# Delta rule: turning values and outputs, and spreading samples' keys, on VectorE, ScalarE and GpSimd instead of TensorE

## The chip, the core and the metric

The program runs on one core of one Trainium2 chip. A core has five engines with a queue each: PE (TensorE, matrix products), DVE (VectorE, elementwise work and 32x32 transposes), ACT (ScalarE, elementwise functions and copies), POOL (GpSimd, elementwise work and some of the DMAs) and SP (SyncE, which here only issues DMAs). Each engine works through its own instructions in the order in which the program issues them and waits, where it has to, for results of the others. The metric is the device time of one execution in microseconds (us); less is better.

## The reference

The program computes one layer of a decoder for one new sequence of 256 tokens (the prompt) and 8 samples of 4 tokens each, 288 tokens together, in float32. What this change touches is the gated delta rule of 8 heads with 128 channels each. For a chunk of tokens with state S, it computes

```
u = T @ (vc * bc)                    # T: inverse of a unit triangular matrix made from keys and decays
w = T @ (kb * jnp.exp(gcum)[..., None])
v_new = u_c - w_c @ S
o = qd @ S + a_c @ v_new
S = S * jnp.exp(gl)[..., None] + jnp.einsum('bhcd,bhce->bhde', kd, v_new)
```

The prompt's 256 tokens are 4 chunks of 64, one after the other. Each of the 8 samples has its own state per head, which its 4 tokens update once. Before and after it stand large matrix products: an input projection (2048 to 11,280 columns), output projections and a feed-forward block with 8192 hidden columns.

## The kernel before

**The stream of blocks.** All large products are cut into 496 blocks of 512 KB of weights (4 groups of 128 rows by 256 columns). Weights in float32 are not multiplied as they are: ACT rounds a block to a shorter format (`split_hi`, L185, tile `hi`), DVE computes what is left over (`split_lo`, L141 by the helper `tt`, tile `lo`), and PE makes three products for each piece (`matmuls`, L211, L212, L214): high by high, high by low, low by high. A block is 24 such products. The main loop goes over blocks i. In iteration i it issues, in this order: `split_hi(i+3)`; one step of the side work, `next(sgen)`; one step of the sample work, `next(aux[0])`; `split_lo(i+3)`; what is due after earlier blocks (`due`: results taken out of PSUM); and then block i's products. `hi` and `lo` have 4 buffers each, so `split_hi(i+3)` can start when PE is done with block i-1.

**Side work.** The delta rule has little arithmetic but a long chain of dependent steps. It is a Python generator, `gdn(G)`, for two groups of 4 heads, G=0 and then G=1. Every `yield` in it ends a step, and one step is issued per block. So the PE instructions of a step stand in PE's queue between block i-1 and block i, and the number of `yield`s between a result and the PE instruction that uses it is written out by hand: it decides how many blocks of PE time the other engines have for it. The samples' part is a second generator inside it, `sample()`, put into `aux` and stepped beside it. When G=0 is through and `aux` is empty, G=1 begins (`side`, L1431 to L1436).

**What gdn does, by lines.** The keys are transposed by PE (L1035), their norms taken, decays made (L1079 to L1102), key-by-key products made (L1111). DVE scales these (`nM`, `aT`). From L1137 to L1144 DVE prepares small 8x8 systems; ACT and POOL split them (`mx`, L1174, L1175); PE sums them (L1181, tile n88); DVE solves them in a chain of about 16 small instructions (L1183 to L1188) and transposes the result (L1189, `Tf`). Three `yield`s later PE begins to merge the blocks into the inverse (`pairs`, L1170, twice for each of two sizes, with ACT's copy L1195 between; then L1208 and L1223), which ends in `U128`. Then comes the loop over the 4 chunks (L1331 to L1372): PE multiplies keys by the state (L1336, p1), DVE subtracts (L144 by the helper `stt`), PE multiplies by `U128` (L1348, p2), DVE scales, PE makes the state's update and the output (L1356 and L1359, p3 and p4), DVE or ACT adds.

**What the change touches in it.** Values lie in `vf` with channels on the partitions and are turned by 8 PE transposes (L1324), with DVE scaling them on the way out of PSUM. The outputs are turned back by 8 PE transposes (L1396), with ACT copies (L1399) into `ao`, which the z blocks read. The sample part needs keys and new values spread to 4 row groups, one for each head: ACT writes the keys 4 times (L1053, `wide`), PE transposes them (L1058) into `kr`; later ACT writes the matrix `Us` 4 times (L1274) and PE makes 4 products from it (L1281). `lows` (L1234 to L1239) rounds such a tile and leaves high or low parts in their row groups. POOL multiplies the samples' states by their decays (L1231, `decay`) and spreads new values with a mask (L1297, `vm`); PE makes the states' updates (L1308).

**Beside it.** While G=0 runs, blocks 24 to 47 produce the keys, queries and values of G=1. After every fourth block a result is due: in the first step after it, and in the next, POOL clears and fills a border (L271, L272), ACT copies out of PSUM (L273, L274) and makes the first product of a convolution of 4 taps (L276, which waits for L272), DVE makes the other three (L144, 128x312), POOL saves a tail (L279). In the third, ACT applies SiLU (L286 to L293). These steps are 28, 29, 30; 32, 33, 34; up to 48, 49, 50. While G=1 runs, the blocks are those of the gated short convolution, with DVE work due in 3 of 12 steps (L141, L144, L344).

```
                act.mul(c, pad[:, 0:312], hw[:, ti, 24:25])
                for j in range(1, 4):
                    stt(c, pad[:, j:j + 312], hw[:, ti, 24 + j:25 + j], c, MUL, ADD)
```

## Time and profile before

| what | value |
|---|---|
| time, median of 3 runs | 1677.83 us (1677.59 to 1677.97) |
| time of the profiled execution | 1677.98 us |
| its span, first to last instruction | 1676.1 us |
| PE busy | 1666.5 us |
| DVE, ACT, POOL busy | 971.6, 733.9, 126.9 us |
| granted TensorE clock | 0.998 |
| G=0, from the first key transposes (L1035) to the output transposes (L1396) on the chain | 80.67 to 251.50 us |
| G=1, the same | 258.87 to 407.37 us |

Times inside the profile count from the first instruction. The chain of waits follows back from the last instruction what each one waited for; a line of it gives start, duration, engine, tile, line and count. The timeline of an engine gives start, duration, line, operation, what is written from what, its shape, and in brackets how long the engine had been idle and who ended that. Groups of instructions give busy time, the mean of one in ns, and idle time before them.

### The profile page before, as it was taken

What the parts mean: (1) busy time and instruction counts of PE and PEld (TensorE: products, weight loads), DVE (VectorE), ACT (ScalarE), POOL (GpSimd) and SP (SyncE); (2) the same over time, 40 slices, a digit from 0 to 9 for tenths busy, and PEclk for the clock granted to TensorE, in tenths of its full rate; (3) what the DMA queues carried; (4) which work ended last, traced back from release to release, by engine and by line L of the source; (5) the groups of instructions that cost most, each with busy time, mean ns of one, the idle gap of its engine ahead of it and who ended that gap; (6) DMA issues with size and microseconds to landing.
All of it is one profiled execution on the core that took longest, in us unless ns stands there. A gap on an engine that the chain in (4) does not pass through costs nothing.

```text
span 1676.1 us, 31314 instructions
## 1 busy us (share of the span) xinstructions
PE 1666.5 (99%) x13245; PEld 1653.1 (99%) x13245; DVE 971.6 (58%) x1244; ACT 733.9 (44%) x1029; POOL 126.9 (8%) x210
## 2 busy tenths in 40 slices
PE   9999999999999999999999999999999999999998
PEld 8999999999999999999999999999999999999997
DVE  5687967676444445457776666544444444444465
ACT  6775545335443333334444445443334433344343
POOL 1223311232200000000000000000000000000000
PEclk9999999999999999999999999999999999999999
DMA  8554466436555555555565555555555555555552
GB/s 274 160 176 152 137 197 189 153 114 201 172 168 167 165 164 163 165 167 162 161 204 165 167 167 163 167 163 164 165 166 167 168 166 164 163 164 166 165 162 83
DMA packets 276035, 279.36 MB, mean 167 GB/s; under 512 B 13779, under 2 KB 270996, under 8 KB 275888
## 3 DMA queue, kind: packets, MB, share of 16 engines
q1 hardware_dynamic: 271782, 265.87, 51.0%
q0 software_dynamic: 3824, 11.16, 2.4%
q8 instruction: 104, 1.70, 0.4%
q10 hardware_dynamic: 288, 0.33, 0.1%
q14 instruction: 37, 0.30, 0.1%
HBM read 269.83 MB, written 7.48 MB: 165 GB/s over the span
## 4 chain that ended last, share of the span: by engine, by line
PE 99%; DMA 1%; DVE 0%; issue 0%; SPq 0%; ACT 0%; POOL 0%
PE acc L211 31%; PE acc L214 31%; PE acc L212 31%; PE g L1170 0%; PE g L1336 0%; DMA xs<-in_x_sample_dram 0%; PE g L1356 0%; PE g L1359 0%; PE g L909 0%; DMA xr<-in_x_prompt_dram 0%; PE g L1161 0%; PE g L1111 0%; PE g L1308 0%; PE g L1348 0%; PE g L1035 0%; PE g L628 0%
## 5 line engine op out<-in xcount | busy, mean ns | idle before, releaser
L141 DVE TENSOR_TENSOR lo<-raw,hi 128x1024 fp32r<-128x1024 f32 (+1 forms) x503 | 614.1, 1224 | 593.4 <-ACT hi L185 592.5
L185 ACT CAST hi<-raw 128x1024 fp32r<-128x1024 f32 (+1 forms) x499 | 519.0, 1042 | 805.4 <-PE acc L212 705.6
L211 PE MATMUL acc<-xh,hi 128*128 128x288 f32 x1408 | 399.4, 299 | 0.3 <-ACT hi L1449 0.3
L212 PE MATMUL acc<-xl,hi 128*128 128x288 f32 x1408 | 394.4, 295 | 0.0
L214 PE MATMUL acc<-xh,lo 128*128 128x288 f32 x1408 | 302.1, 295 | 0.0
L212 PE MATMUL acc<-dl,hi 128*128 128x288 f32 (+1 forms) x1024 | 287.7, 295 | 0.0
L211 PE MATMUL acc<-dh,hi 128*128 128x288 f32 (+1 forms) x1024 | 287.6, 295 | 0.0
L211 PE MATMUL acc<-hh,hi 128*128 128x288 f32 x1024 | 287.4, 295 | 0.0
L212 PE MATMUL acc<-hl,hi 128*128 128x288 f32 x1024 | 287.2, 295 | 0.0
L211 PEld LDWEIGHTS acc<-xh,hi 128*128 128x128 f32 x1408 | 264.6, 188 | 2.5 <-issue 1.0
L212 PEld LDWEIGHTS acc<-xl,hi 128*128 128x128 f32 x1408 | 264.6, 188 | 0.9
L214 PEld LDWEIGHTS acc<-xh,lo 128*128 128x128 f32 x1408 | 226.0, 188 | 0.0
L214 PE MATMUL acc<-hh,lo 128*128 128x288 f32 x1024 | 222.6, 296 | 0.0
L214 PE MATMUL acc<-dh,lo 128*128 128x288 f32 (+1 forms) x1024 | 219.8, 296 | 0.0
L211 PEld LDWEIGHTS acc<-dh,hi 128*128 128x128 f32 x1024 | 193.3, 189 | 0.1
L212 PEld LDWEIGHTS acc<-dl,hi 128*128 128x128 f32 x1024 | 192.8, 188 | 0.1
L211 PEld LDWEIGHTS acc<-hh,hi 128*128 128x128 f32 x1024 | 192.4, 188 | 0.0
L212 PEld LDWEIGHTS acc<-hl,hi 128*128 128x128 f32 x1024 | 192.2, 188 | 0.0
L214 PEld LDWEIGHTS acc<-hh,lo 128*128 128x128 f32 x1024 | 165.1, 188 | 0.0
L214 PEld LDWEIGHTS acc<-dh,lo 128*128 128x128 f32 x1024 | 164.6, 188 | 0.0
L211 PE MATMUL acc<-mh,hi 128*128 128x288 f32 x256 | 72.1, 298 | 0.0
L212 PE MATMUL acc<-ml,hi 128*128 128x288 f32 x256 | 71.7, 295 | 0.0
(414 smaller groups left out, 1479.8 us busy)
## 6 DMA issues: line engine op xcount, KB each, us to landing
raw<-in_w_in_dram SPq DMA_DIRECT2D x175, 512.0 KB, 3.5
raw<-in_w_up_dram SPq DMA_DIRECT2D x128, 512.0 KB, 3.7
raw<-in_w_down_dram SPq DMA_DIRECT2D x128, 512.0 KB, 3.5
raw<-in_w_o_dram SPq DMA_DIRECT2D x32, 512.0 KB, 3.6
raw<-in_w_a_out_dram SPq DMA_DIRECT2D x16, 512.0 KB, 3.6
raw<-in_w_b_out_dram SPq DMA_DIRECT2D x16, 512.0 KB, 3.6
S<-in_state_gdn_dram POOLq DMA_DIRECT2D x8, 512.0 KB, 6.4
out_dram<-S POOLq DMA_DIRECT2D x8, 512.0 KB, 4.7
```

Source lines behind the costliest of these rows:

```text
L141: dve.tensor_tensor(out=out, in0=a, in1=b, op=op)
L185: act.copy(his[i][:, k:k + step], raw[i][:, k:k + step])
L211: pe.matmul(ps[:, t, 0:n], wh, xh_, start=st, stop=False)
L212: pe.matmul(ps[:, t, 0:n], wh, xl_, start=False, stop=False)
L214: pe.matmul(ps[:, t, 0:n], l[:, k, t * P:(t + 1) * P], xh_, start=False, stop=en)
```

## The change

1. **Values.** The 8 PE transposes and 2 DVE products after the sample part's start are gone. Right after L1111, DVE turns `vf` in 32x32 blocks in one instruction (128x1024) into the room of `U128`; ACT moves the blocks to their places in 16 copies (32x256), four in each of four steps (`move_v`); DVE scales all in one 128x1024 product, just ahead of n88. The clearing of `U128` by POOL moves behind that.
2. **Outputs.** DVE turns `o` in one 128x1024 instruction, ACT moves it in 16 copies (32x256), eight in each of two steps.
3. **Keys of the samples.** `wide`, its 4 PE transposes, the norms of the fourfold tile and its factors (`srep`, `rsc`) are gone; `kr` is one 128x128 tile copied from a transpose that was there already.
4. **Spreading.** `lows`, the second `wide` and the 4 PE products are gone. `quarters` rounds the tile (ACT), takes the rest (DVE), and copies 16 pieces (32x128) to their row groups: all 16 by POOL for the keys; for the new values 8 by POOL and 8 by ACT.
5. **Steps.** The `sample` generator gets longer by two steps up to its `po` and its pieces move among them; one step between the merge matrix `Us` and its use is gone. The chunk loop starts one step earlier in both groups and, for G=0, loses the extra `yield` after each chunk. So G=0 ends, and G=1 starts, five steps earlier.

```diff
+        v = T([P, 4, 2, P], "v")
+        vt = U128.rearrange("p q x -> p (q x)")
+        dve.transpose(out=vt, in_=vf.rearrange("p r c a x -> p (r c a x)"))
+        vtv = vt.rearrange("p (r c a e) -> p c r a e", r=2, c=4, a=4)
+        def move_v(j):
+            for w in range(4):
+                act.copy(v[32 * w:32 * w + 32, :, :, 32 * j:32 * j + 32], vtv[32 * j:32 * j + 32, :, :, w])
...
-        yield
+        move_v(0)
+        yield
+        move_v(1)
...
         gps.tensor_tensor(out=mx[:, 1], in0=Xf, in1=mx[:, 0], op=SUB)
+        move_v(2)
         yield
         spread_kq(1)
-        yield
+        move_v(3)
+        yield
+        vq = v.rearrange("p c r x -> p (c r) x")
+        tt(vq, vq, bc(nr[:, 0:8], P), MUL)
+        gps.memset(U128, 0.0)
         n88 = gtile()
...
+        def quarters(out, src, side_):
+            act.copy(hl[:, 0], src)
+            tt(hl[:, 1], src, hl[:, 0], SUB)
+            for hh in range(4):
+                for w in range(4):
+                    low = w // 2 if side_ == 0 else w % 2
+                    d, r = out[32 * w:32 * w + 32, hh], hl[32 * hh:32 * hh + 32, low]
+                    if side_ and w % 2:
+                        act.copy(d, r)
+                    else:
+                        gps.tensor_copy(d, r)
+                if hh % 2:
+                    yield
...
             dve.transpose(out=Ts, in_=Us)
             yield
-            yield
+            yield from quarters(kr3, kr, 0)
...
             dve.copy_predicated(Us, msk("s"), pqs[:, 0:P])
-            lows(kr3, kr, 0)
-            yield
-            act.copy(wide, four(Us))
             yield
             pv_ = gtile()
             pe.matmul(pv_[:, 0:P], Us, vs, start=True, stop=True)
             act.mul(vns, pv_[:, 0:P], sc[:, 1:2])
-            vtr = gtile()
-            for hh in range(4):
-                pe.matmul(vtr[:, hh * P:hh * P + P], rep4[:, hh * P:hh * P + P], vs, start=True, stop=True)
-            vr = sqr[:, 0:512].rearrange("p (h d) -> p h d", h=4)
-            tt(vr, vtr.rearrange("p (h d) -> p h d", h=4), bc(rsc[:, 1], P), MUL)
             v3 = pl.tile([P, 4, P], F32R, tag="U", name=nm("v3"))
-            lows(v3, vr, 1)
+            yield from quarters(v3, vns, 1)
...
-        for u in range(2):
-            vt = gtile()
-            for w in range(4):
-                pe.transpose(vt[:, w * P:(w + 1) * P], vf[:, w % 2, 2 * u + w // 2].rearrange("p a x -> p (a x)"), ident)
...
             yield
-            if G == 0:
-                yield
         gps.dma_start(A["new_gdn_prompt"][0, 0, hs].rearrange("h d e -> d h e"), S)
...
+        ot = v.rearrange("p c r x -> p (c r x)")
+        dve.transpose(out=ot, in_=o.rearrange("p c r x -> p (c r x)"))
+        otv = ot.rearrange("p (c r j x) -> p j r c x", c=4, r=2, j=4)
         yield
+        for w in range(4):
+            for j in range(4):
+                h = 4 * G + 1 - w // 2
+                ao = gd["ao"][32 * j:32 * j + 32, 1, h:4 * G + 4:2, 0:NP_].rearrange("p r (c t x) -> p t r c x", c=4, t=2)
+                act.copy(ao[:, w % 2], otv[32 * w:32 * w + 32, j])
+            if w == 1:
+                yield
```

More of the change, by code (lines that the diff above doesn't have):

```diff
@@ L972, in gates @@
                 gps.tensor_copy(gw[64 - 64 * par:128 - 64 * par, half], qv[src, par, 0])
-        srep = cp.tile([P, 2, 8], F32, name="srep")
-        act.activation(srep[:, 0], q[:, 136:144], AF.Exp)
-        act.copy(srep[:, 1], q[:, 144:152])
         s4 = cp.tile([P, 4, 8], F32, name="s4")
@@ L984, in gates @@
         dve.tensor_scalar(out=sx[:, 3, :], in0=s1[:, 0, :], scalar1=-1.0, scalar2=None, op0=MUL)
-        G_.update(srep=srep, eg=gpt[:, 0], kd=gpt[:, 1], ngc=gpt[:, 2], neg=gpt[:, 3], beta=gpt[:, 4], g=gpt[:, 5], egs=gsw,
+        G_.update(eg=gpt[:, 0], kd=gpt[:, 1], ngc=gpt[:, 2], neg=gpt[:, 3], beta=gpt[:, 4], g=gpt[:, 5], egs=gsw,
                   egl=ge[:, 0:32].rearrange("p (b h c) -> p b h c", b=2, c=2),
@@ L990, in gates @@
         yield
-    def four(ap):
-        return ap.rearrange("p (h t) -> p h t", h=4).unsqueeze(2).to_broadcast([P, 4, 4, 32])
     def gdn(G):
@@ L1016, in gdn @@
         sqr = T([P, 1024], "vmh")
-        rep4 = sqr[:, 512:1024]
         junk = sqr[:, 192:320]
-        wide = rep4.rearrange("p (h q t) -> p h q t", h=4, q=4)
         U128 = T([P, 8, P], "U128")
@@ L1024, in gdn @@
         gl = T([P, 4, 2, 64], "gl")
-        ss = T([P, 22], "ss")
+        ss = T([P, 18], "ss")
         red = T([P, 4, 4], "red")
@@ L1051, in gdn @@
         pe.transpose(sp2[:, 128:256], qst, ident)
-        act.copy(wide, four(kst))
         states_in(1)
         yield
-        ktr = gtile()
-        for hh in range(4):
-            pe.transpose(ktr[:, hh * P:hh * P + P], rep4[:, hh * P:hh * P + P], ident)
-        kr = T([P, 4, P], "kr")
+        kr = T([P, P], "kr")
         for u in range(2):
             act.activation(junk, sp2[:, u * P:u * P + P], AF.Square, accum_out=ss[:, 16 + u:17 + u])
-        act.copy(kr, ktr.rearrange("p (h d) -> p h d", h=4))
-        act.activation(sqr[:, 0:512], ktr, AF.Square)
-        dve.tensor_reduce(out=ss[:, 18:22], in_=sqr[:, 0:512].rearrange("p (h d) -> p h d", h=4),
-                          axis=mybir.AxisListType.X, op=ADD)
+        act.copy(kr, sp2[:, 0:P])
         states_in(2)
@@ L1075, in gdn @@
         yield
-        gps.memset(U128, 0.0)
         gr = gtile()
@@ L1079, in gdn @@
             pe.matmul(gr, hmr, glx[:, u], start=(u == 0), stop=(u == 1))
-        nr = T([P, 22], "nr")
-        rn = T([P, 22], "rn")
+        nr = T([P, 18], "nr")
+        rn = T([P, 18], "rn")
         act.activation(nr, ss, AF.Sqrt, bias=epsc[:, 1:2])
@@ L1091, in gdn @@
         sc = T([P, 4], "sc")
-        rsc = T([P, 2, 4], "rsc")
         srk, snk = rn[:, 16:17], nr[:, 16:17]
-        tt(rsc, G_["srep"][:, :, hs], bmid(rn[:, 18:22], 2), MUL)
+        tt(sc[:, 0:1], G_["s_kd"][:, G:G + 1], srk, MUL)
         tt(sc[:, 1:2], G_["s_beta"][:, G:G + 1], srk, MUL)
@@ L1233, in gdn @@
         kr3 = pl.tile([P, 4, P], F32R, tag="kr3", name=nm("kr3"))
-        def lows(out, src, side_):
-            hi = pl.tile([P, 4, P], F32R, tag="gl", name=nm("hi4"))
-            act.copy(hi, src)
-            stt(out, hi, cst("nlow")[:, side_:side_ + 1], src, MUL, ADD)
+        hl = pl.tile([P, 2, P], F32R, tag="kr2", name=nm("hl"))
+        def quarters(out, src, side_):
[11 more added lines that the diff above has]
+                    yield
         def sample():
@@ L1250, in sample @@
             act.mul(vs, sp1[:, 384:512], snk)
-            gps.tensor_tensor(out=kr, in0=kr, in1=bc(rsc[:, 0], P), op=MUL)
+            act.mul(kr, kr, sc[:, 0:1])
             stt(nMs, sp1[:, 0:128], sc[:, 2:3], Es, MUL, MUL)
@@ L1278, in sample @@
             act.mul(vns, pv_[:, 0:P], sc[:, 1:2])
-            vtr = gtile()
-            for hh in range(4):
-                pe.matmul(vtr[:, hh * P:hh * P + P], rep4[:, hh * P:hh * P + P], vs, start=True, stop=True)
-            vr = sqr[:, 0:512].rearrange("p (h d) -> p h d", h=4)
-            tt(vr, vtr.rearrange("p (h d) -> p h d", h=4), bc(rsc[:, 1], P), MUL)
             v3 = pl.tile([P, 4, P], F32R, tag="U", name=nm("v3"))
-            lows(v3, vr, 1)
+            yield from quarters(v3, vns, 1)
             yield
@@ L1319, in gdn @@
         aux.append(sample())
-        v = T([P, 4, 2, P], "v")
-        for u in range(2):
-            vt = gtile()
-            for w in range(4):
-                pe.transpose(vt[:, w * P:(w + 1) * P], vf[:, w % 2, 2 * u + w // 2].rearrange("p a x -> p (a x)"), ident)
-            tt(v[:, 2 * u:2 * u + 2].rearrange("p c r x -> p (c r) x"), vt.rearrange("p (q x) -> p q x", q=4),
-               bc(nr[:, 4 * u:4 * u + 4], P), MUL)
-        yield
         S = T([P, 4, P], "E")
@@ L1390, in gdn @@
         act.mul(osm, osm, so[:, 8:9])
+        ot = v.rearrange("p c r x -> p (c r x)")
+        dve.transpose(out=ot, in_=o.rearrange("p c r x -> p (c r x)"))
+        otv = ot.rearrange("p (c r j x) -> p j r c x", c=4, r=2, j=4)
         yield
-        yield
-        for u in range(2):
-            pt = gtile()
-            for w in range(4):
-                pe.transpose(pt[:, w * P:(w + 1) * P], of[:, 4 * u + w, :], ident)
-            pv = pt.rearrange("p (c r s x) -> p s c r x", c=2, r=2, s=2)
-            for par in range(2):
-                act.copy(gd["ao"][:, 1, 4 * G + par:4 * G + 4:2, P * u:P * u + P].rearrange("p r (c x) -> p c r x", c=2),
-                         pv[:, 1 - par])
+        for w in range(4):
[5 more added lines that the diff above has]
+                yield
         yield
```

## Prediction

> **What bounds the kernel now.** I read the page first (busy times, then the chain that ended last), then the waits and the timelines.

> ```profile
> PE 1666.5 (99%) x13245; PEld 1653.1 (99%) x13245; DVE 971.6 (58%) x1244; ACT 733.9 (44%) x1029; POOL 126.9 (8%) x210
> ...
> PE 99%; DMA 1%; DVE 0%; issue 0%; SPq 0%; ACT 0%; POOL 0%
> ```

> ```profile
> PE g L801 <- DVE warm L796: 1.2, 1, 1.2
> ```

> ```profile
> 238.53 1.05 ACT L185 CAST hi<-raw 128x1024 fp32r<-128x1024 f32 x1 [3.43 <-PE acc L212]
> 241.71 1.05 ACT L185 CAST hi<-raw 128x1024 fp32r<-128x1024 f32 x1 [2.13 <-PE acc L212]
> ```

> PE has 99% of the chain, ACT's roundings wait for PE, and PE's own longest wait for another engine is 1.2 us, at the start. So whatever leaves PE's queue is won, and whatever makes PE wait is lost. Two roundings, each of which waits for the end of a block, lie 3.18 us apart: that is a block without side work, and what one `yield` gives the other engines.

> **What PE no longer does.** The chain in order of time has each removed group; here G=0's four and the last of G=1's, which repeat them:

> ```profile
> 92.19 0.44 PE g L1058 x4
> ...
> 163.37 0.87 PE g L1324 x8
> ...
> 184.24 0.89 PE g L1281 x8
> ...
> 251.50 0.87 PE g L1396 x8
> ...
> 407.37 0.87 PE g L1396 x8
> ```

> 0.44 + 0.87 + 0.89 + 0.87 = 3.07 us a group, **6.1 us** for both. Nothing is added on PE. One transpose in a row of eight costs 0.87/8 = 0.109 us.

> [...]

> **What the others get.** Prices, from DVE's groups and from the timelines of ACT and POOL:

> ```profile
> L1200 DVE STREAM_TRANSPOSE U<-U 128x256 f32<-128x256 f32 x4 | 1.8, 446 | 0.1
> ...
> L144 DVE SCALAR_TENSOR_TENSOR v<-g,gpt,v 64x128 f32<-64x128 f32 x24 | 8.4, 349 | 4.1 <-PE g L1336 3.8
> ...
> L1256 DVE STREAM_TRANSPOSE b<-b 128x128 f32<-128x128 f32 x2 | 0.6, 312 | 0.1
> ```

> ```profile
> 160.08 0.73 ACT L1225 COPY U<-g 32x256 f32<-32x256 f32 x2
> ```

> ```profile
> 151.51 2.66 POOL L1213 COPY U<-U 32x256 f32<-32x256 f32 x4 [7.72 <-DVE U L1199]
> 154.23 0.52 POOL L1217 COPY vmh<-vmh 128x128 f32<-128x128 f32 x2
> ```

> 128 more elements cost a turn 0.134 us, so 1024 take 0.446 + 6 x 0.134 = 1.25 us (at most 4 x 0.446 = 1.8). The scaling of 128x1024 is like a `lo` (1.23 us, below). An ACT copy is 0.365 us: 2.9 us for eight. A POOL copy of 128 elements is 0.26 us, more when it must wait. The outputs' part I cost at nothing: its 16 ACT copies (5.8 us in two steps, with two roundings of 1.05) exceed the two steps by about 1.5 us, and roundings are made three blocks ahead, which covers it (without that: 1.5 us a group). `kr`, one tile instead of four, only shortens ACT's steps.

> **Values: the chain to n88 and L1170 in G=0.** DVE, then ACT, then PE:

> ```profile
> 104.66 0.29 DVE L1083 RECIPROCAL rn<-nr 128x22 f32<-128x22 f32 x1 [1.26 <-ACT nr L1082]
> ...
> 123.23 0.69 DVE L141 TENSOR_TENSOR xt<-vmh,cf 128x512 f32<-128x512 f32 x1
> ...
> 129.38 1.70 DVE L144 SCALAR_TENSOR_TENSOR w<-w,hw 128x312 f32<-128x312 f32 x3 [0.91 <-ACT w L276]
> ```

> ```profile
> 128.79 0.56 ACT L276 ACTIVATE w<-w,hw 128x312 f32<-128x312 f32 x1 [2.91 <-POOL w L272]
> ...
> 140.53 0.36 ACT L1195 COPY xt<-g 128x256 f32<-128x256 f32 x1
> ```

> ```profile
> 141.12 0.68 PE g L1170 x50
> ...
> 305.22 0.47 PE g L1181 x2
> ```

> Between the two brackets on DVE, from 104.66 on, it had no gap, and the turn is put into that stretch. What follows `xt` (123.92) is one chain: the split by ACT and POOL, POOL's copies, the border that L276 waited 2.91 us for, DVE's convolution, the small system and its turn, the next convolution, SiLU, two roundings, and L1195, which ends at 140.89. PE's second L1170 starts at 141.12: 0.2 us of slack. The turn adds 1.25 ahead of `xt`, the scaling 1.23 behind the first convolution and ahead of the small system. The eight copies of the third and fourth `move_v` (2.9 us) fill the 2.91 us that ACT waits there; I add 0.2. Together 2.7 less the slack: PE waits **2.5 us** (2.9 if the copies overrun by 0.4 more; 1.2 if one of the two finds a gap).

> **The same chain in G=1.** It starts five steps earlier and so meets a convolution of the other kind on DVE:

> ```profile
> 267.38 1.01 DVE L141 TENSOR_TENSOR w<-acc,hs 128x512 f32<-128x512 f32 x3
> ...
> 270.06 0.36 DVE L344 TENSOR_SCALAR w<-w,hwa 128x304 f32<-128x304 f32 x1
> 270.46 1.11 DVE L144 SCALAR_TENSOR_TENSOR w<-w,hwa,w 128x304 f32<-128x304 f32 x2
> ```

> ```profile
> 296.97 0.69 DVE L141 TENSOR_TENSOR xt<-vmh,cf 128x512 f32<-128x512 f32 x1
> ```

> ```profile
> 300.27 1.81 POOL L1175 TENSOR_TENSOR mx<-xt,mx 128x512 fp32r<-128x512 f32 x1 [24.74 <-ACT mx L1174]
> ```

> Added: 1.25 + 1.01 + 2 x 1.47 = 5.2. Slack: `xt` ends at 297.66 and POOL's half starts at 300.27, of which ACT's half is 0.6, so 2.0; that ends at 302.08 and PE asks at 305.22, 3.1. I take **0.5 us** (0 to 2.4).

> **The chunk loop in G=0.** Here a wait is added behind which much is queued. POOL's 16 copies of the keys are issued in steps 43 and 44, ahead of step 44's border, L272. ACT's L276 waits for L272, DVE's convolution for L276, and behind that in DVE's queue stand step 45's four subtractions (L144, 64x128, 0.349 each), for which step 46's p2 on PE waits.

> Count from PE's arrival at step 42 (163.2 before):

> ```profile
> 175.25 0.65 PE g L1356 x8
> 175.90 0.64 PE g L1359 x4
> ...
> 183.12 0.89 PE g L1336 x8
> ```

> ```profile
> 163.10:173.50 10.40, 10.40 (x84) 10.40 (x84) 9.36 (x13) 7.17 (x13) 4.43 (x4) 1.00 0.17 52
> ```

> PE: step 42 is p2 0.44, seven passes of 0.109, a block 3.18, 4.4 us; step 43, 3.2; step 44, p3 and p4 1.29 and a block, 4.5; step 45, p1 0.89, 0.22 and a block, 4.3. So p2 is due at **16.4**. ACT (the fifth number of the row of that stretch, 7.17) works through the same instructions as before up to the new copy `hl`, less one rounding of 1.0, with a product of about 0.4 added: the first POOL copy can start at 6.6. The 16 take 16 x 0.27, and two wait out a `lo` (1.1 each): 13.1; the border is there at 13.4, L276 ends at 14.0. Then POOL's decays start, together with the three convolution products:

> ```profile
> 116.39 1.73 DVE L144 SCALAR_TENSOR_TENSOR w<-w,hw 128x312 f32<-128x312 f32 x3
> ...
> 171.74 0.41 DVE L141 TENSOR_TENSOR v<-g,brk 128x256 f32<-128x256 f32 x1
> 172.45 1.23 DVE L141 TENSOR_TENSOR lo<-raw,hi 128x1024 fp32r<-128x1024 f32 x1 [0.30 <-ACT hi L185]
> 173.60 0.34 DVE L144 SCALAR_TENSOR_TENSOR b<-kso,sx,b 128x128 f32<-128x128 f32 x1
> ...
> 174.99 4.77 DVE L144 SCALAR_TENSOR_TENSOR w<-w,hw 128x312 f32<-128x312 f32 x3
> ```

> ```profile
> 175.11 4.30 POOL L1231 TENSOR_TENSOR S<-S,gexp 128x1024 f32<-128x1024 f32 x2
> ```

> Beside two decays the three products took 4.77 us instead of 1.73. So the convolution ends at 14.0 + 4.8 = 18.8, the first two subtractions at 19.5, p2 starts at 19.7: PE waits **3.3 us** (1.0 if no copy waits, 3.9 if four do).

> p2 ends at 20.6 with the last subtraction. After one product more and a block PE asks for `pv_` at 24.0. It needs `Us`, made by a DVE instruction of step 46 (the step between is gone). DVE has, from 20.2: two products 0.85, one 0.34, `lo` 1.23, the next convolution 1.73, p2's scaling 0.41, its own 0.3, that is 25.1, and one wait for a decay (2.15): 27.2. PE waits **3.2 us** (1.0 without the decay). G=1 has no such border in these steps; there the same count brings `Us` as PE asks.

> With the `yield` after a chunk gone, p1 comes one block after p3 instead of two:

> ```profile
> 198.89 1.11 DVE L144 SCALAR_TENSOR_TENSOR E<-E,gexp,g 128x128 f32<-128x128 f32 x4
> ```

> In chunk 1 the state was done at 200.0, p3 and p4 had ended at 196.7, one block later is 199.9; I add **0.3 us** (0 to 1.0).

> **The sum.** -6.1 + 2.5 + 0.5 + 3.3 + 3.2 + 0.3 = +3.7 us on the profiled execution (span 1676.1, time 1677.98): 1681.7. That execution is 0.15 above the median of the three runs, so **1681.5**. All low ends: -6.1 + 1.2 + 0 + 1.0 + 1.0 + 0 = -2.9 (1674.9); all high ends: -6.1 + 2.9 + 2.4 + 3.9 + 3.4 + 1.0 = +7.5 (1685.3).

> **The rivals.**
> *Border in time.* If step 44's border comes by 10.1 (13.4 - 3.3), p2 finds its values, and DVE is early enough for `pv_` too. That decides the sign: the copies would have to start near 3.3 instead of 6.6, or the decays not fall on the convolution. Then -6.1 + 2.5 + 0.5 + 0.3 = -2.8: 1675.0, not slower. For it: POOL is busy 8% and often runs ahead. Against it: seven us of ACT's work stand in front, and the row above shows decays on the convolution.
> *All hidden.* The n88 chain finds gaps too: -6.1, 1671.7. Against it: 0.2 us of slack at L1170.
> *PE slows down after a wait.* If a wait of 3 us made PE lose half its clock for one block, 3.2 us more would go for each of the two waits: 1681.5 + 6.4 = 1687.9. Against it: the granted clock is 1.00 in the row of the stretch above, with no wait that long anywhere to test it. [...]

> **How the numbers follow.** Forecast 0.62 (its own range 1677 to 1685.3; 0.42 of it above +0.2%, 0.20 within); border in time 0.20 (0.15 within 0.2%, 0.05 faster); all hidden 0.10, faster; slow clock 0.08, slower. 0.2% (3.4 us, about what a measurement of this kernel can tell from no change) lies at 1674.5 and 1681.2. So faster 0.15, same 0.35, slower 0.50. The range that leaves out 0.2 reaches from 1673.0, between the hidden case and the timely border, to 1686.5, short of the slow clock.

> **What would show it.** In the profile after: L1058, L1281, L1324 and L1396 gone from PE; waits of PE for DVE of 2 to 4 us at p2 (L1348) and `pv_` (L1288) in G=0, and at L1170 or L1181; ACT's L276 waiting for POOL's L272; the convolution's L144 long beside decays. If PE's waits stay under 0.5 us each, the chunk loop was misread and the time is 1672 to 1675. If the turn takes over 1.8 us, or POOL's copies between row groups over 0.5 us each, it is slower than I say.

## The result, and the profile after

The changed kernel takes **1680.67 us** (median of 20 runs, 1680.42 to 1681.16), the kernel before 1677.91 us (20 runs, 1677.55 to 1678.12): 2.76 us more, a ratio of 1.0017 with a 95% interval from 1.0011 to 1.0023. The prediction was 1681.5 with a range from 1673.0 to 1686.5.

The page of the profiled execution (1680.53 us, span 1678.4), its busy times and the chain that ended last:

```profile
PE 1663.6 (99%) x13189; PEld 1648.7 (98%) x13189; DVE 970.2 (58%) x1242; ACT 757.0 (45%) x1094; POOL 139.2 (8%) x256
...
PE 95%; DVE 2%; ACT 1%; DMA 1%; issue 1%; POOL 0%; SPq 0%; ACTq 0%; DVEq 0%; POOLq 0%
```

PE issues 56 products less, as counted, but is no longer the whole chain: DVE and ACT have taken shares of it. What PE waited for (waiting line, releaser; total, times, longest):

```profile
PE g L1342 <- DVE v L144: 3.6, 1, 3.6
PE g L1164 <- ACT xt L1194: 1.3, 1, 1.3
PE g L801 <- DVE warm L796: 1.2, 1, 1.2
PE g L1164 <- DVE U L1188: 1.1, 1, 1.1
PE g L750 <- PE acc L699: 0.9, 1, 0.9
PE g L1284 <- DVE b L1281: 0.5, 1, 0.5
```

L1164 is `pairs` (L1170 before), L1342 is p2, L1284 is `pv_` (the samples' product of `Us` with their values). All four new waits lie in G=0. The waits say nothing of PE's pace. That is in the stretches from p2's start on. A row gives the stretch and its length, the busy time of PE, weight loads, DVE, ACT and POOL, the granted clock, and two columns on DMA:

```profile
185.86:187.70 1.84, 1.74 (x7) 1.45 (x8) 1.81 (x5) 0.68 (x3) 1.84 (x2) 0.56 0.00 0
187.70:189.45 1.75, 1.75 (x9) 1.75 (x8) 1.75 (x2) 0.00 (x0) 1.03 (x1) 0.50 0.00 0
189.45:192.20 2.75, 2.32 (x17) 2.08 (x16) 2.68 (x7) 0.54 (x3) 0.00 (x0) 0.99 0.37 98
```

Behind p2's wait PE ran at half its clock for 3.4 us (0.50 from 186.09 to 189.51). The rows of p2 and `pv_` in PE's timeline give the cost:

```profile
185.86 1.45 PE L1342 MATMUL g<-v,U 128*128 128x128 f32 x4 [3.64 <-DVE v L144]
187.10 0.64 PE L1280 MATMUL g<-b 128*128 128x128 f32 x2
192.22 0.49 PE L1284 MATMUL g<-b 128*128 128x128 f32 x2 [0.45 <-DVE b L1281]
```

From p2's start to the end of block 46 it took 192.22 - 0.45 - 185.86 = 5.91 us; at the full clock, with all inputs there, it is 0.44 + 0.22 + 3.18 = 3.84. So **2.1 us** went there. Not all of it is the clock's: p2's later products also wait for DVE's later subtractions. The run `filled` below, which has the same p2 at the full clock, puts about 1.3 us on the clock and 0.8 on these.

A smaller wait stands inside n88, whose second product needs POOL's half of the split (L1169, done at 126.92):

```profile
126.44 1.03 PE L1180 MATMUL g<-mx,bo 128*128 128x512 f32 x2
127.31 0.29 PE L211 MATMUL acc<-xh,hi 128*128 128x288 f32 x1
```

From n88 to the next product it takes 0.87 us here, and 0.47 in the row of n88 that the prediction shows: 0.4 us more.

**The account.** -6.1 for the products, +0.4 inside n88, +2.4 for the two waits at `pairs`, +3.6 at p2, +2.1 for the stretch behind it, +0.5 at `pv_`: +2.9, and some tenths where products behind a wait take longer (`pv_`'s two 0.49 us in the row above, two of L1254 without a wait 0.39, at 166.14). The chain's pieces near the end bear it out. Before and after:

```profile
1663.38 1.31 PE acc L695 x12
```

```profile
1666.60 1.31 PE acc L695 x12
```

That is +3.2 us up to there; in this execution the last results then landed sooner (2.5 us from issue, 3.3 before), which fits that the spans differ by 2.3 alone.

### The profile page after: what moved, and what is told of

Its sections match the earlier page's. It is cut to its first block, busy times and chain, and to the rows that moved or that the text cites. A ratio compares the mean times of both kernels' runs of the same rounds, so it can differ in the third digit from the quotient of the medians.

```text
span 1678.4 us, 31304 instructions
## 1 busy us (share of the span) xinstructions
PE 1663.6 (99%) x13189; PEld 1648.7 (98%) x13189; DVE 970.2 (58%) x1242; ACT 757.0 (45%) x1094; POOL 139.2 (8%) x256
## 4 chain that ended last, share of the span: by engine, by line
PE 95%; DVE 2%; ACT 1%; DMA 1%; issue 1%; POOL 0%; SPq 0%; ACTq 0%; DVEq 0%; POOLq 0%
PE acc L211 30%; PE acc L214 30%; PE acc L212 30%; DVE w L144 1%; POOL kr L1247 0%; ACT hi L185 0%; DVE lo L141 0%; DMA xs<-in_x_sample_dram 0%; PE g L1164 0%; PE g L1350 0%; PE g L1353 0%; PE g L1330 0%; PE g L909 0%; PE g L1155 0%; DMA xr<-in_x_prompt_dram 0%
## 5 line engine op out<-in xcount | busy, mean ns | idle before, releaser
L141 DVE TENSOR_TENSOR lo<-raw,hi 128x1024 fp32r<-128x1024 f32 (+1 forms) x503 | 612.8, 1222 | 595.7 <-ACT hi L185 594.7
L185 ACT CAST hi<-raw 128x1024 fp32r<-128x1024 f32 (+1 forms) x499 | 519.2, 1043 | 783.3 <-PE acc L212 687.3
L212 PE MATMUL acc<-xl,hi 128*128 128x288 f32 x1408 | 395.0, 295 | 0.0
L212 PE MATMUL acc<-dl,hi 128*128 128x288 f32 (+1 forms) x1024 | 287.8, 296 | 0.0
L212 PE MATMUL acc<-hl,hi 128*128 128x288 f32 x1024 | 287.3, 295 | 0.0
L212 PEld LDWEIGHTS acc<-xl,hi 128*128 128x128 f32 x1408 | 265.2, 188 | 0.9
L212 PEld LDWEIGHTS acc<-dl,hi 128*128 128x128 f32 x1024 | 192.9, 188 | 0.1
L212 PEld LDWEIGHTS acc<-hl,hi 128*128 128x128 f32 x1024 | 192.3, 188 | 0.0
L212 PE MATMUL acc<-ml,hi 128*128 128x288 f32 x256 | 71.7, 295 | 0.0
```

The source lines that it names most:

```text
L141: dve.tensor_tensor(out=out, in0=a, in1=b, op=op)
L185: act.copy(his[i][:, k:k + step], raw[i][:, k:k + step])
L212: pe.matmul(ps[:, t, 0:n], wh, xl_, start=False, stop=False)
```

## The experiments

Each result is set against the kernel before on the same chip, as a difference of medians (for the change itself: +2.76). A ratio is against that kernel too, with its 95% interval.

### What makes p2 wait: the place of the key copies

`keys_early` makes the key copies in steps 34 and 35:

```diff
         dve.transpose(out=Tf, in_=Uf)
-        for _ in range(3):
-            yield
...
+        yield
+        act.mul(kr, kr, sc[:, 0:1])
+        act.copy(hl[:, 0], kr)
+        gps.tensor_tensor(out=hl[:, 1], in0=kr, in1=hl[:, 0], op=SUB)
+        for hh in range(4):
+            for w in range(4):
+                gps.tensor_copy(kr3[32 * w:32 * w + 32, hh], hl[32 * hh:32 * hh + 32, w // 2])
+            if hh % 2:
+                yield
...
-            act.mul(kr, kr, sc[:, 0:1])
...
-            yield from quarters(kr3, kr, 0)
+            yield
+            yield
```

> The changed kernel with one thing moved: the samples' keys are scaled, rounded and copied to their row groups (16 POOL copies) ten steps earlier, behind the start of the 8x8 solve, and the two steps in which POOL made them stay empty. Theory A (the 16 copies ahead of step 44's border cause p2's wait in G=0): the border comes some 4 us earlier, p2's wait falls from 3.7 us to under 0.7, PE's slow passage after it (2.0 us) goes with it, the wait at the new values' product stays under 1.0, the waits of 2.4 us behind the 8x8 solve stay: 1674.2 to 1675.5 us. Theory B (the shortened chunk loop and the decays beside the convolution cause it, whoever is ahead in POOL's queue): p2 still waits 1.5 us or more, 1678 or more.

Measured: 1676.66 against 1678.19, **-1.53**, ratio 0.9991 (0.9982 to 1.0000): against the kernel before at the edge of the noise, but 4.3 us less than the change. PE's waits in G=0:

```profile
PE g L1289 <- DVE b L1286: 1.8, 1, 1.8
PE g L1164 <- ACT xt L1203: 1.3, 1, 1.3
PE g L1164 <- DVE U L1188: 1.2, 1, 1.2
```

```profile
176.69 4.50 DVE L144 SCALAR_TENSOR_TENSOR w<-w,hw 128x312 f32<-128x312 f32 x3 [0.68 <-ACT w L276]
181.10 1.45 DVE L144 SCALAR_TENSOR_TENSOR v<-g,gpt,v 64x128 f32<-64x128 f32 x4
...
183.25 1.73 DVE L144 SCALAR_TENSOR_TENSOR b<-kso,sx,b 128x128 f32<-128x128 f32 x1
```

p2's wait is gone and the slow stretch with it, although the convolution beside the decays is as long as ever (4.50 us): theory A on p2. Theory A's time was missed by about 1 us, because `pv_` (L1289 here) now waits 1.8 us, where it expected under 1.0. The last row points at the cause: one 128x128 product that takes 0.34 us by itself takes 1.73 beside a decay. `keys_mid` below tests that.

`decays_early` leaves the copies and takes the decays away from the convolution:

```diff
             dve.transpose(out=Ts, in_=Us)
+            for hh in range(2):
+                decay(hh)
             yield
             yield from quarters(kr3, kr, 0)
-            for hh in range(2):
-                decay(hh)
```

> The changed kernel with the first two decays issued in step 42, ahead of the key copies, instead of step 45, so that they don't lie beside step 44's convolution. If copies and decays share the blame for p2's wait as the prediction counted (border late by the copies, three products 4.4 us long instead of 1.75 beside the decays): p2's wait falls by 2.7 to about 1.0 us, PE's slow passage (2.0 us) goes, the next wait (new values' product) grows from 0.5 to 1.2 to 2.5: 1676.5 to 1677.8 us. If the late border alone decides: no change, 1680.7. If two more decays ahead of the copies delay these as much as they spare: 1680 or more.

Measured: 1679.73 against 1678.19, **+1.54**, ratio 1.0009 (1.0000 to 1.0018). POOL, then DVE:

```profile
164.39 4.03 POOL L1230 TENSOR_TENSOR S<-S,gexp 128x1024 f32<-128x1024 f32 x2
174.30 7.17 POOL L1247 CAST kr<-hl 32x128 fp32r<-32x128 f32 x16 [5.88 <-ACT hl L1238]
```

```profile
182.50 1.70 DVE L144 SCALAR_TENSOR_TENSOR w<-w,hw 128x312 f32<-128x312 f32 x3 [5.49 <-ACT w L276]
184.12 1.45 DVE L144 SCALAR_TENSOR_TENSOR v<-g,gpt,v 64x128 f32<-64x128 f32 x4
```

The three products are back at 1.70 us. But the decays now lay on DVE's and, through it, ACT's work of step 42, so the copies started 1.6 us later, counted from PE's arrival at step 42 (8.2 us instead of 6.6). p2 still waited 2.4 us, and PE still went through a half-clock stretch. The expected 1.0 was wrong by that delay, and the time with it (1676.5 to 1677.8 expected). Together the two runs say: without the late border p2 doesn't wait, even with the decays beside the convolution; with it, the decays stretch what stands behind it. Both have a share in the 3.6 us.

`keys_mid` does both: keys in steps 38 and 39, all four decays in steps 42 and 43. In its edit `keys(h0)` stands for the eight POOL copies of two heads.

```diff
             act.copy(Xc, px[:, 0:256].rearrange("p (q c) -> p q c", q=8))
+            if s == 16:
+                act.mul(kr, kr, sc[:, 0:1])
+                act.copy(hl[:, 0], kr)
+                gps.tensor_tensor(out=hl[:, 1], in0=kr, in1=hl[:, 0], op=SUB)
+                keys(0)
             yield
...
             states_of(s // 16)
+            if s == 16:
+                keys(2)
             yield
...
             dve.transpose(out=Ts, in_=Us)
+            for hh in range(2):
+                decay(hh)
             yield
-            yield from quarters(kr3, kr, 0)
-            for hh in range(2):
-                decay(hh)
+            for hh in range(2, 4):
+                decay(hh)
+            yield
+            yield
...
-            for hh in range(2, 4):
-                decay(hh)
```

> The changed kernel with the samples' keys spread in steps 38 and 39 and with all four decays issued in steps 42 and 43, so that neither copies nor decays lie beside the convolution and the subtractions of steps 44 to 46. If the wait of 1.8 us at the new values' product, which was left when only the copies were moved, comes from the decays beside DVE's instructions of steps 45 and 46: it falls to under 0.5, p2 doesn't wait, the 2.4 us behind the 8x8 solve stay, and the time is 3.2 to 3.7 us below that of the kernel before on the same chip. If it comes from the shortened loop: 1.5 us or more stay, and the time is 1.2 to 2.0 below.

Measured: 1674.58 against 1678.03, **-3.45**, ratio 0.9979 (0.9970 to 0.9988). Of the new waits only those at `pairs` are left:

```profile
PE g L1164 <- ACT xt L1202: 1.3, 1, 1.3
PE g L1164 <- DVE U L1188: 1.1, 1, 1.1
```

So `pv_`'s wait belonged to the decays in steps 45 and 46, not to the shortened loop, which is unchanged here. The time is as its first theory had it.

### What makes the merges wait: DVE's turn and scaling

`scale_late` moves only the scaling, behind the last turn of the merges (`if s == 16`, after `states_of`):

```diff
-        vq = v.rearrange("p c r x -> p (c r) x")
-        tt(vq, vq, bc(nr[:, 0:8], P), MUL)
         gps.memset(U128, 0.0)
...
             states_of(s // 16)
+            if s == 16:
+                vq = v.rearrange("p c r x -> p (c r) x")
+                tt(vq, vq, bc(nr[:, 0:8], P), MUL)
```

> The changed kernel with DVE's scaling of the values (128x1024) moved from ahead of the 8x8 solve to behind the last turn of the merges. If it stands in the chain to the merges with its whole 1.23 us: the first of the two waits there (1.1 us) goes, the second (1.3) stays, since the convolution ahead of it moves with PE's arrival: 1679.2 to 1679.6 us. If both waits hang on it: 1678.2. If the solve is held by ACT's moves or POOL's clearing instead: 1680.5 or more.

Measured: 1679.86 against 1678.19, **+1.67**, ratio 1.0010 (1.0001 to 1.0019), so 1.1 us less than the change; the first wait is gone, the second stays at 1.3, as the first theory had it (the kernel before is 0.3 us slower on this chip than where the change was measured, and the time 0.3 above the theory's range).

`values_late` also moves the turn to step 32 and the moves to steps 33 to 36:

```diff
-        move_v(0)
         yield
-        move_v(1)
...
         spread_kq(1)
-        move_v(3)
+        dve.transpose(out=vt, in_=vf.rearrange("p r c a x -> p (r c a x)"))
         yield
+        move_v(0)
...
-        for _ in range(3):
+        for j in range(1, 4):
             yield
+            move_v(j)
```

> The changed kernel with the turn of the values put where DVE waited for the border's first product (step 32), the 16 moves behind it, the clearing of U128 in step 37 and the scaling behind the merges: nothing of the values' part is left in the chain to the 8x8 solve. If the turn (1.24 us) and the scaling (1.23) are what PE waited 2.4 us for: no wait of over 0.3 us at the merges in either group, 1677.8 to 1678.4 us; p2's wait of 3.7 stays. If the work only moves to another stretch (a wait at the later merges, or at the first p2): 1679.5 or more.

Measured: 1683.51 against 1678.19, **+5.32**, ratio 1.0032 (1.0020 to 1.0045): a miss. PE's first wait went, but the second grew to 3.5 us (`L1161 <- ACT xt L1189`), and a stretch at half clock came behind it (granted clock 0.50 from 144.35 to 147.76; the mean over the whole execution was 0.996, in the change 0.998). ACT's timeline:

```profile
138.23 0.42 ACT L291 ACTIVATE kq<-w 128x256 f32<-128x256 f32 x1 [3.15 <-DVE w L144]
138.56 0.22 ACT L293 ACTIVATE kqs<-w 128x32 f32<-128x32 f32 x1
138.68 1.04 ACT L185 CAST hi<-raw 128x1024 fp32r<-128x1024 f32 x1
139.74 1.64 ACT L1102 COPY v<-U 32x256 f32<-32x256 f32 x4
141.41 1.04 ACT L185 CAST hi<-raw 128x1024 fp32r<-128x1024 f32 x1
142.47 1.64 ACT L1102 COPY v<-U 32x256 f32<-32x256 f32 x4
144.14 0.37 ACT L1189 COPY xt<-g 128x256 f32<-128x256 f32 x1
```

ACT stands in the SiLU (L291) until DVE's convolution ends. Two sets of moves queued behind it, and ahead of the copy that PE waits for. The moves had to be ahead of the SiLU, not behind it.

`all_free` is keys_mid with that mended: turn in step 32, two sets of moves in each of steps 33 and 34, `U128` cleared in step 37, scaling as in scale_late.

```diff
         spread_kq(1)
+        dve.transpose(out=vt, in_=vf.rearrange("p r c a x -> p (r c a x)"))
         yield
+        move_v(0)
+        move_v(1)
...
         yield
+        move_v(2)
+        move_v(3)
+        yield
+        yield
```

> As keys_mid, and besides the values turned by DVE in step 32, moved by ACT in steps 33 and 34 ahead of the SiLU that ACT waits in, scaled behind the merges. All of PE's saving (6.1 us) then stands with no added wait of over 0.5 us: 5.2 to 6.1 us below the kernel before on the same chip. If ACT's moves still hold the copy between the two merge products (as with values_late): a wait of 1 to 3 us there, 2 to 4.5 below.

Measured: **1671.38** against 1678.03, **-6.65**, ratio 0.9960 (0.9948 to 0.9973): faster than both kernels. Its chain:

```profile
PE 99%; DVE 0%; issue 0%; ACT 0%
```

PE waits nowhere in either group, so all of its 6.1 us stand: the piece `PE acc L695 x12`, at 1663.38 before, starts at 1657.31 here, 6.07 earlier. In the profiled execution another 0.3 us is gained behind that piece; the cause of what lies beyond the 6.1 stays open.

### The outputs' part alone

`outputs_only` is the kernel before with that part (its lines as in the change):

```diff
+        ot = v.rearrange("p c r x -> p (c r x)")
+        dve.transpose(out=ot, in_=o.rearrange("p c r x -> p (c r x)"))
+        otv = ot.rearrange("p (c r j x) -> p j r c x", c=4, r=2, j=4)
         yield
-        yield
-        for u in range(2):
-            pt = gtile()
...
+        for w in range(4):
+            for j in range(4):
...
```

> The kernel before with the outputs' part of the change alone: 16 PE transposes (0.87 us a group) less, one turn on DVE and 16 ACT copies a group in the two steps. If ACT's copies stand beside other work, as the prediction counted them: 1.7 us below the kernel before, no wait of PE. If 5.8 us of ACT copies in two steps hold back ACT's roundings: a wait of PE for them of up to 1.5 us a group, 1.3 above to 1.0 below.

Measured: 1677.72 against 1678.03, **-0.31**, ratio 0.9998 (0.9989 to 1.0007). In G=1 there is one wait:

```profile
PE g L1058 <- ACT vmh L1053: 1.4, 1, 1.4
```

Neither theory: the roundings are in time, but ACT's copies (3.3 us for eight, 0.41 each) leave it without a gap into the next group, so that `wide` (L1053), which the kernel before still has at the start of G=1, is late for PE's transposes of it: it starts at 270.40, before at 268.32. The 1.4 us take back most of the 1.7 of the 16 transposes. In the whole change `wide` is gone and PE has no wait there. The parts don't add up one by one.

### The half clock

`waits` and `short_waits` put waits of graded length into PE's queue of the kernel before, away from all side work:

```diff
+    def stall(n):
+        g1 = gtile()
+        pe.transpose(g1[0:64, 0:P], ident[:, 0:64], ident)
+        act.copy(wt[0:64, 0], g1[0:64, 0:64])
+        for k in range(n):
+            act.copy(wt[0:64, 1 - k % 2], wt[0:64, k % 2])
+        g2 = gtile()
+        pe.transpose(g2[0:64, 0:64], wt[0:64, n % 2], ident[0:64, 0:64])
+    for k in range(16):
+        at(170 + 12 * k, lambda k=k: stall(k % 8 + 1))
```

(`waits`: POOL copies in the middle, nine places.)

> The kernel before with nine waits of graded length put into PE's queue, 20 blocks apart, in the stretch without side work (a transpose, an ACT copy, 3 to 19 POOL copies of 64x64, a transpose that needs the last). If PE goes slower after a wait only from some length on: the blocks behind the short waits take 3.2 us as ever, and those behind the long ones have a stretch of some 3.6 us in which a product comes every 0.24 us instead of 0.133, costing 1.6 to 2.0 us; from the runs so far the bound lies between 1.75 and 2.4 us. If the slow stretch belongs to the place (a short product after the wait, or the side work): no slow stretch here at any length.

Measured: 1747.03 (one run), PE waiting 48.6 us in nine waits of 2.7 to 7.5 us, each followed by a stretch in which a product comes every 0.24 us instead of 0.133; the mean granted clock was 0.982, in the kernel before 0.998. Behind the wait of 2.7 us the clock was 0.50 from 621.0 to 624.3. So it belongs to the wait, not to the place; but even the shortest was too long to show a bound.

> The kernel before with sixteen shorter waits put into PE's queue, 12 blocks apart (a transpose, 2 to 9 ACT copies of 64x64, a transpose that needs the last), twice each length, from about 1 to 2.7 us. If length decides: no slow stretch behind waits of up to 1.8 us, a stretch at a granted clock of 0.5 behind those of 2.4 and more, and the change from one to the other somewhere between at one length. If it depends on where in a fixed period the wait falls: waits of one length with and without a slow stretch, and some of the slow stretches behind waits of under 1.8 us.

Measured: 1742.61 (one run), at a mean granted clock of 0.986. Waits of 1.1 to 1.5 us (four) were followed by the full clock, those of 2.6 us and more (seven) by the half. Between, length doesn't decide: 1.70 and 1.97 us half, 1.74, 2.02 and 2.28 full. Stretches cut every 3.413 us, at the times at which the granted clock changes in this execution; the first three hold the wait of 1.97 us, the last three that of 2.28:

```profile
1079.96:1083.38 3.42, 1.45 (x12) 1.09 (x10) 1.47 (x3) 2.13 (x6) 0.00 (x0) 1.00 0.52 156
1083.38:1086.79 3.41, 3.41 (x15) 3.41 (x15) 2.17 (x4) 0.00 (x0) 0.00 (x0) 0.50 0.52 154
1086.79:1090.20 3.41, 3.41 (x28) 3.41 (x27) 1.01 (x1) 2.06 (x4) 0.00 (x0) 1.00 0.00 0
...
1120.92:1124.34 3.42, 2.66 (x21) 2.37 (x19) 1.90 (x2) 1.81 (x4) 0.00 (x0) 1.00 0.57 179
1124.34:1127.75 3.41, 1.89 (x14) 1.82 (x15) 1.23 (x1) 1.31 (x6) 0.00 (x0) 1.00 0.54 164
1127.75:1131.16 3.41, 3.41 (x28) 3.41 (x27) 0.80 (x1) 1.05 (x1) 0.00 (x0) 1.00 0.27 92
```

The shorter wait lay in one stretch, with 3.42 - 1.45 = 1.97 us without PE, and the next stretch was at 0.50. The longer one was cut in two, 0.76 and 1.52 us, and nothing followed. That is the second theory: of these two it was not the longer one that was followed by the half clock, but the one that lay in a single stretch of 3.41 us.

`filled` asks whether the slow stretch cost the change any time. It gives PE 28 transposes of a constant, into a part of p2's tile that nobody reads, to do in p2's wait:

```diff
             p2 = gtile()
+            if G == 0 and c == 1:
+                for _ in range(28):
+                    pe.transpose(p2[:, 384:512], ident, ident)
```

> The changed kernel with 28 transposes of a constant, which nobody reads, put ahead of chunk 1's second product (p2) in G=0: about 3.05 us of PE work in a wait of 3.64, so that PE is not idle there. No half-clock stretch should follow. Theory A (DVE's chain sets when the new values' product can start, and the slow stretch only took the place of a wait for it): the wait at the new values' product grows from 0.5 to 2 to 2.6 us and the time stays that of the changed kernel, 2.4 to 3.0 us above the kernel before on the same chip. Theory B (the slow stretch adds its own 2.0 us): 0.5 to 1.0 above it.

Measured: 1682.26 against 1678.09, +4.17, ratio 1.0022 (1.0013 to 1.0031), above the times of both theories, but in two heaps: 4 of the 11 runs from 1680.76 to 1680.88, 7 from 1682.11 to 1682.38. The profiled execution is of the upper heap:

```profile
182.26 3.22 PE L1343 MATMUL g<-cf 128*128 128x128 f32 x28
186.00 0.49 PE L1345 MATMUL g<-v,U 128*128 128x128 f32 x2 [0.52 <-DVE v L144]
186.75 0.49 PE L1345 MATMUL g<-v,U 128*128 128x128 f32 x2 [0.26 <-DVE v L144]
...
192.46 0.49 PE L1284 MATMUL g<-b 128*128 128x128 f32 x2 [1.82 <-DVE b L1281]
```

From p2 to `pv_` it takes 192.46 - 186.00 = 6.46 us, in the change 192.22 - 185.86 = 6.36: PE's full clock moved nothing, the wait at `pv_` only grew to 1.8. So theory A holds for the chain, and the lower heap (+2.7) has theory A's time. PE itself was done with the block at 192.46 - 1.82 = 190.64, 4.64 us after p2's start, in the change after 5.91: so the half clock took 1.3 us of PE's time, and the other 0.8 above 3.84 come from p2's later products, which wait for subtractions at the full clock too (the 0.26 above).

What a half-clock stretch took beyond the wait in whose place it came was lost. In the profiled execution of scale_late the stretch behind the same p2 wait lasted twice as long (6.8 us, the first 0.9 still inside the wait), `pv_` did not wait at all, and p2 to `pv_` took 6.78 us, 0.4 more than in the change; the mean granted clock was 0.996, in the change 0.998. In that of `filled` the wait of 1.8 us is followed by a half-clock stretch of its own, with no wait behind it (granted clock 0.54 over the 3.4 us), which fits the 1.5 us between the heaps; that the runs of the lower heap lack it was not seen in a profile and stays an inference.

## Why the prediction was right, step by step

The forecast was +3.7 us, the result +2.8, and the place that decides, p2, came as told. The time lies below 1681.2, so in the prediction's class "same" (0.35) and not in "slower" (0.50), though the interval shows a loss of 0.1 to 0.2%. Some terms missed, and that the sum came so near is in part luck: 0.5 in G=1 and 0.3 at a chunk's end didn't come, 0.4 inside n88 was not forecast, and the term of the values holds two errors that nearly cancel.

**PE's saving: right.** -6.1 us; with all waits taken away (all_free) nothing of it is missing.

**The chain to n88 and L1170 in G=0: right in its sum** (2.5 forecast, 1.1 + 1.3 at `pairs` measured, besides the 0.4 inside n88). DVE's two new rows (mean ns of one behind the busy time), and the first convolution's:

```profile
L1098 DVE STREAM_TRANSPOSE U<-vf 128x1024 f32<-128x1024 f32 x2 | 2.5, 1234 | 0.0
L141 DVE TENSOR_TENSOR v<-v,nr 128x1024 f32<-128x1024 f32 x2 | 2.5, 1229 | 0.4 <-ACT v L1103 0.4
...
130.85 1.71 DVE L144 SCALAR_TENSOR_TENSOR w<-w,hw 128x312 f32<-128x312 f32 x3 [1.50 <-ACT w L276]
```

1.25 and 1.23 were forecast. The convolution starts 1.5 us later than before (129.38), as forecast (1.25 + 0.2), but by other shares: PE, and DVE with it, were 0.4 us ahead by then, so `xt` came only 0.7 later (123.93, before 123.23); the eight moves took 3.3 us instead of 2.9 and held L276 some 0.8 us beyond the border (done at 129.41, L276 at 130.26). scale_late shows that the scaling stood in the chain; that the turn did was argued from all_free, which moves it with other things.

**G=1: 0.5 forecast, nothing measured,** within its bounds (0 to 2.4): POOL's half of the split took 1.56 us instead of 1.81 and ended at 294.58, PE asked at 294.96.

**p2: right** (3.3 forecast, 3.6 measured). POOL, ACT and DVE in the change:

```profile
172.33 7.31 POOL L1247 CAST kr<-hl 32x128 fp32r<-32x128 f32 x16 [8.27 <-ACT hl L1238]
...
179.84 0.20 POOL L272 COPY w<-hw 128x24 f32<-128x24 f32 x1
...
180.08 0.56 ACT L276 ACTIVATE w<-w,hw 128x312 f32<-128x312 f32 x1 [4.57 <-POOL w L272]
...
180.67 4.42 DVE L144 SCALAR_TENSOR_TENSOR w<-w,hw 128x312 f32<-128x312 f32 x3 [5.15 <-ACT w L276]
185.01 1.45 DVE L144 SCALAR_TENSOR_TENSOR v<-g,gpt,v 64x128 f32<-64x128 f32 x4
```

Counted from 165.70, where PE came to step 42, the copies began at 6.6 as forecast, and took 7.3 us instead of 6.5 (two of them 1.2 and 1.3 us beside a `lo`, close to the forecast 1.1; the others came every 0.33 us, not 0.27), the border was there at 14.3 (13.4), DVE was through with the convolution at 19.4 (18.8), p2 began at 20.2 (19.7). In the rival "border in time" the point from which it decides was right too: in keys_early the border is in time and p2 doesn't wait. But that rival gave `pv_` away, which there still waited 1.8. The high end of 3.9, for four copies that wait, doesn't follow from its own price: two more at 1.1 us would have made 5.5.

**`pv_`: 3.2 forecast, 0.5 measured; its chain on DVE was nearly right, PE's arrival was not.** `Us` was to come at 27.2 and came at 26.5. PE did not ask at 24.0 but at 26.1, for the most part because it had been at half clock (1.3 us; p2 itself began 0.5 later than forecast). At the full clock, in `filled`, the wait is 1.8, so the term was 1.4 too large even there; its high end of 3.4 is nowhere worked out. The rival "PE slows down after a wait" came true in its mechanism, once; its price was wrong: it had 3.2 us, on top of the waits, where 1.3 came, in the place of one. p2's wait, the slow stretch and `pv_`'s wait together are 6.2 us, against 3.3 + 3.2 = 6.5 forecast without it. That is no luck: `Us` sets when PE goes on at `pv_`, however PE loses the time before, and only how this time is shared out was wrong.

**The end of a chunk: 0.3 forecast, nothing measured** (its low end).

**The outputs and `kr`: right for this change,** for a reason that the prediction did not give: outputs_only shows that the copies do delay ACT into the next group, where PE waits for `wide`; the change has no `wide`.

## What to carry to other kernels

Work taken from an engine that is always busy is a gain only where what replaces it stands outside the chains which that engine waits for. Here 6.1 us were there to be had, and three places in hand-written queues (turn, moves and scaling of the values ahead of a solve, copies ahead of a border, decays beside a convolution) turned them into a loss of 2.8; the same instructions some steps earlier or later gave a gain of 6.65. Before moving work onto an in-order queue, look for the instruction there that will stand blocked (ACT in its SiLU) and for the one that others wait for (POOL's border), and put the new work ahead of the first and behind the second.

## What the runs showed of the hardware

Two kinds of DVE products with both inputs in SBUF became 2.6 and 5 times longer beside POOL's decays: three of 128x312 took 4.42 us in the change instead of 1.70 (decays_early), one of 128x128 took 1.73 in keys_early instead of 0.34 (the kernel before). The 64x128 subtractions, whose one input lies in PSUM, did not: four took 1.45 us beside a decay (185.01 in the change), and 1.46 in the kernel before with POOL idle (184.42).
